# DeltaNet inverses by 8x8 blocks, stored by row, with all their multiplications on VectorE

## The chip, the core and the metric

The kernel runs on one core of one Trainium2 chip. A core has five engines with queues of their own: TensorE (PE in the profile; PEld are its weight loads), VectorE (DVE), ScalarE (ACT), GpSimd (POOL) and SyncE (SP, which issues the loads). Each engine works through its queue in order and waits at semaphores for the others. The metric is the device time of one execution in microseconds (us); the median over runs counts.

## The reference

Two layers, each made of a feed-forward network, a mixer and a second feed-forward network, over 256 tokens of width 1024. The mixer has three kinds of heads: window attention (6), differential attention (4) and a gated delta rule (6, in both directions). The change is in the delta rule alone. For each head, direction and chunk of 64 tokens it solves a unit lower triangular system:

```python
m_low = jnp.where(tril_strict, jnp.einsum('bhncd,bhnsd->bhncs', kb, kc) * decay, 0.0)
a_mat = jnp.eye(C, dtype=f32) + m_low
u = lax.linalg.triangular_solve(a_mat, vb, left_side=True, lower=True, unit_diagonal=True)
w = lax.linalg.triangular_solve(a_mat, kb * jnp.exp(gc)[..., None], left_side=True,
                                lower=True, unit_diagonal=True)
```

With 6 heads, 2 directions and 4 chunks there are 48 matrices of 64x64 in each layer.

## The kernel before

The kernel does not solve the systems; it inverts the matrices. Each 64x64 matrix is cut into two diagonal blocks of 32x32 and one block below them. The 96 diagonal blocks of a layer are laid one to a partition (four groups of 32 partitions, 24 used in each), so that one VectorE instruction works on all of them. `inv_start` gathers them into Dg, partly with VectorE's 32x32 transpose and partly with ScalarE copies, and transposes Dg into L; Vi is to become the inverse. Every step of the inversion is a call of `products`: one multiplication (TENSOR_TENSOR, line 799) of two broadcast views into the scratch tile pr, and one reduction over its last dimension (TENSOR_REDUCE, line 800). Each needs the one before.

- `inv_row` (ORDER's "ir"): the two 16x16 diagonal blocks of the 32x32, row by row, i = 1 to 15. Step i multiplies 2·i·i elements.
- `inv_off` ("io", n = 0 to 5): the block below them, by products of 1024 elements: three of L with Vi into pp, three of Vi with pp into Vi.
- `inv_end` ("ie"): transposes and copies of the result into WA and W, which TensorE then uses to complete the 64x64 inverse (`off1`, `off2`) and to run the scan over chunks.

L holds a block so that going along the summed index steps by 32 elements; Vi is read along consecutive elements in the row steps and in the first three "io" steps.

The set SHARED names the operations that go to GpSimd instead of VectorE: of the inversion the multiplications of rows 2, 4 and 11 (v2, v4, v11) and of the fifth "io" step (u4). Others in the set are additions of the convolution (t1, t7, t8, line 548) and of the differential heads (d0 to d3, line 729).

The table ORDER says in which order the mixer's pieces are written down; a scheduler then merges them into the queues, so that an engine's order is near to the table but not the same. Around the inversion stand: "p:9" to "p:16", projections for the attention heads, each of 8 matmuls (line 428, tile pj); "d", differential scores (lines 708 and 713, tile pss); "w", window scores (lines 669 and 675, also pss); "h" and "hw", heads' outputs. Projections and scores are written into the same pool of two PSUM buffers, "pm". A projection's buffer is free when VectorE has taken it out (dqk line 662, wq line 659). A differential score's buffer is free when VectorE has taken its maximum (mxd, line 716) and ScalarE has read it through two exponentials (line 719). Weights come by SyncE loads, up to seven ahead of their use.

Of the kernel before, what the change touches and what calls it, by code (L numbers as in the profile page):

```python
# [35 lines left out]
ORDER = """  # L36
A:0 A:1 A:2 K N A:3 G V c:1:0 c:1:1 clear c:0:0 c:1:2 GS co:1:0 c:0:1 co:1:1 co:1:2 ce:1 GE GT E:1 qn:1 co:0:0 co:0:1
c:0:2 co:0:2 ce:0 qn:0 E:0 E:3 qc:1:1 c:2:0 c:2:1 E:2 qc:0:0 qc:1:0 X:0:0 qc:0:1 ic X:1:1 X:0:1 X:1:0 i ir:1:2 ir:2:3
ir:3:4 ir:4:5 ir:5:6 p:15 ir:6:7 ir:7:8 ir:8:9 ir:9:10 ir:10:11 ir:11:12 ir:12:13 ir:13:14 c:2:2 ir:14:15 p:14 p:13
co:2:0 p:16 d:0 ir:15:16 d:2 co:2:1 io:0 co:2:2 p:9 d:1 p:12 d:3 w:0 io:1 h:2 h:1 p:10 h:0 io:2 io:3 h:3 p:11 w:1 w:2  # L40
hw:0 io:4 io:5 ie ce:2 dn hw:1 f g:0 hw:2 g:1 sa:0 sb:0 oT:3:4 sc:0 sa:1 sb:1 sc:1 sa:2 sb:2 sc:2 sa:3 sc:3 z:0 z:1
z:2 z:3 ze on:1 o:0:0 on:0 o:0:1 o:0:2 o:0:3 o:0:4 o:0:5 o:0:6 oT:7 oT:5:6 o:0:7 o:1:0 o:1:1 o:1:2 o:1:3 o:1:4 o:1:5
o:1:6 o:1:7
"""

NRAW = 8
# [3 lines left out]
    p2="pt", pk="pd", px="pt", pS="pt", po="pd", pw="pd", pT="pd", pso="pd", pto="pd",  # L50
)

SHARED = set("O2 S2 d0 d1 d2 d3 g5 s3 t1 t7 t8 u4 v11 v2 v4 x0 x4 x5".split())
C_M0, C_M1, C_DD, C_WD, C_SEL = 0, 64, 128, 640, 1152
NCONSTB = 1176

# [1 line left out]
class Kernel:  # L58
# [296 lines left out]
    def mixer(self, l, gnext):  # L355
# [22 lines left out]
        with ExitStack() as ctx:  # L378
# [4 lines left out]
            st = {}  # L383
# [13 lines left out]
            oT = tile_([P, KD, S], "oT")  # L397
# [130 lines left out]
            def conv(a, b):  # L528
# [15 lines left out]
                act(cv, pad[:, 0:S], AF.Copy, scale=cw[:, i * 5 : i * 5 + 1])  # L544
                if f"t{i}" in SHARED:
                    tap = self.sp.tile([P, S], F32, tag="sqt", name="tap")
                    act(tap, pad[:, 1 : S + 1], AF.Copy, scale=cw[:, i * 5 + 1 : i * 5 + 2])
                    gtt(cv, cv, tap, ALU.add)
                for w in range(2 if f"t{i}" in SHARED else 1, 5):
                    stt(cv, pad[:, w : w + S], cw[:, i * 5 + w : i * 5 + w + 1], cv, ALU.mult, ALU.add)  # L550
                st["cv", a, b] = cv

            def conv_out(a, b):
# [6 lines left out]
                cs = mt.tile([P, S], F32, tag="cs", name="cs")  # L560
                pool = f"s{a * 3 + b}" in SHARED
                if pool:
# [32 lines left out]
            def qk_channels(a, p):  # L595
# [4 lines left out]
                for e in range(2):  # L600
                    for half in range(2):
                        (nc.vector.tensor_copy if ("kq", a, half) in SHARED else nc.scalar.copy)(
                            kq[HALF[half], p, e:6:2, 1 - a, :],
# [60 lines left out]
            def win_scores(b):  # L664

                banks = [bank("pss") for j in range(2)]
                for j, pss in enumerate(banks):
                    if f"g{j * 3 + b}" in SHARED:
                        mm(pss, lhsT=self.wdiag[j * 3 + b], rhs=self.wd.rearrange("p a t -> p (a t)"), start=True, stop=False)
                for p in range(2):  # L670
                    c = slice(p * P, (p + 1) * P)
                    for j, r in enumerate(HALF):
                        slope = f"g{j * 3 + b}" in SHARED
                        o = banks[j][:, p * S : (p + 1) * S]
# [114 lines left out]
            def blk(t, off, *dims):  # L789

                base = t.rearrange("p a b -> p (a b)")
                return bass.AP(
                    tensor=base.tensor, offset=base.offset + off, ap=[list(base.ap[0])] + [list(x) for x in dims]
                )

            def products(o, in0, in1, dims, neg, on):
                n = dims[0] * dims[1] * dims[2]
                pv = st["pr"][:, 0:n].rearrange("p (a c j) -> p a c j", a=dims[0], c=dims[1])
                (gtt if on in SHARED else tt)(pv, in0, in1, ALU.mult)
                nc.vector.tensor_reduce(o, pv, AX.X, ALU.add, negate=neg)  # L800
# [8 lines left out]
            def inv_start():  # L809
                Dg = st["Dg"]  # L810
                for v in range(2):
                    us = slice(v * 12, v * 12 + 12)
                    for b in range(4):
                        o_ = Dg[B32[b], :, us].rearrange("p c u -> p u c")
                        if (b < 2) == (v == 0):
                            nc.vector.transpose(o_, XE[B32[b], 0, us, B32[b % 2]])
                        else:
                            act(o_, XE[B32[b], 0, us, B32[b % 2]], AF.Copy)
                L = st["L"] = tile_([P, 32, 32], "L", "t4b")
                nc.vector.transpose(L, Dg)  # L820
                st["pr"] = tile_([P, 1024], "pr", "pr")
                st["pp"] = tile_([P, 16, 16], "pp")

            def inv_row(i0, i1):
                Vi, L = st["Vi"], st["L"]
                for i in range(i0, i1):
                    products(
                        blk(Vi, i, (528, 2), (32, i)),
                        blk(L, i, (528, 2), (0, i), (32, i)),
                        blk(Vi, 0, (528, 2), (32, i), (1, i)),  # L830
                        (2, i, i),
                        True,
                        f"v{i}",
                    )

            def inv_off(n):
                Vi, L, pp = st["Vi"], st["L"], st["pp"]
                if n < 2:
                    i0 = n * 8
                    products(  # L840
                        pp[:, i0 : i0 + 8, 0:8],
                        blk(L, 16 + i0, (1, 8), (0, 8), (32, 16)),
                        blk(Vi, 0, (0, 8), (32, 8), (1, 16)),
                        (8, 8, 16),
                        False,
                        f"u{n}",
                    )
                elif n == 2:
                    products(
                        pp[:, :, 8:16],  # L850
                        blk(L, 16 + 8 * 32, (1, 16), (0, 8), (32, 8)),
                        blk(Vi, 8 * 33, (0, 16), (32, 8), (1, 8)),
                        (16, 8, 8),
                        False,
                        f"u{n}",
                    )
                elif n == 3:
                    products(
                        blk(Vi, 16, (1, 8), (32, 16)),
                        blk(Vi, 528, (1, 8), (0, 16), (32, 8)),  # L860
                        blk(pp, 0, (0, 8), (1, 16), (16, 8)),
                        (8, 16, 8),
                        True,
                        f"u{n}",
                    )
                else:
                    c0 = (n - 4) * 8
                    products(
                        blk(Vi, 24 + c0 * 32, (1, 8), (32, 8)),
                        blk(Vi, 528 + 8, (1, 8), (0, 8), (32, 16)),  # L870
                        blk(pp, c0, (0, 8), (1, 8), (16, 16)),
                        (8, 8, 16),
                        True,
                        f"u{n}",
                    )
# [142 lines left out]
            def out_proj(part, d):  # L1018
# [20 lines left out]
                "clear": clear, "N": norm, "V": values, "G": gates, "GS": gate_sums, "GE": gate_exps, "GT": gate_rows,  # L1039
                "c": conv, "co": conv_out, "ce": conv_end, "qn": qk_norm, "qc": qk_channels,  # L1040
                "E": decay, "X": products_kq, "K": constants, "p": att, "hw": win_out, "w": win_scores, "d": diff_scores, "h": head_out,
                "dn": diff_norm, "oT": to_oT, "ic": inv_clear, "i": inv_start, "ir": inv_row, "io": inv_off, "ie": inv_end,
                "f": off1, "g": off2, "ze": gate_out, "sa": scan_a, "sb": scan_b, "sc": scan_c, "on": out_norm, "o": out_proj,
                "l": load, "A": lambda a: token_proj(NA, "pv", "A", a),
                "z": lambda a: token_proj(NB, "pz", "z", a),
# [3 lines left out]
            for item in ORDER.split():  # L1049
                w = item.split(":")  # L1050
# [4 lines left out]
                elif w[0] == "o":  # L1055
                    n = (5, 3)[int(w[1])]
# [6 lines left out]
            for item, rs in zip(ORDER.split(), reads):  # L1063
# [6 lines left out]
                w = item.split(":")  # L1070
# [165 lines left out]
```

## Time and profile before

| what | value |
|---|---|
| median of 3 runs | 1150.33 us (1150.1 to 1151.57) |
| profiled execution | 1153.34 us, of which span 1151.5 us |
| PE busy | 1110.3 us (96%) |
| DVE busy | 738.0 us (64%) |
| ACT busy | 522.9 us (45%) |
| POOL busy | 82.3 us (7%) |
| mean granted TensorE clock | 0.977 |
| layer 0's mixer, inversion from first product to Vc | 262.84 to 309.95 us |
| layer 1's, the same | 826.45 to 873.55 us |

Times in the views count from the span's start. A row of a timeline has start, duration, engine, source line, operation, output and inputs, and in brackets how long the engine was idle before and who ended that. A row of groups has count, busy us, mean ns and idle before. A row of stretches has the busy time of each engine, the granted clock of TensorE (1.00 is full speed) and what the loads moved. The matmul records of 32-bit data come in pairs: a projection of 8 matmuls shows 16.

### The profile page before, as it was taken

Reading aid. Unit: us, or ns where it says so; the run is one execution under the profiler, and the core shown is the slowest. Engines: PE = TensorE matmul, PEld = TensorE weight load, DVE = VectorE, ACT = ScalarE, POOL = GpSimd, SP = SyncE. Lnnn points to the kernel's source line nnn. Section 1 sums busy time; section 2 is a strip of 40 time slices with the busy share of each in tenths; the row PEclk is TensorE's granted clock in tenths of the full one; section 3 lists DMA queues with packets and bytes.
Section 4 is the critical chain, followed back from the end, with each engine's and each line's share of the span. In section 5 each row is a group of like instructions: output and inputs, shape, how many; then the busy total and the mean of one; then the engine's idle time right before and its main releaser. Section 6 shows DMA issues by size and latency. Waiting matters only on the chain. (4 is left out here: it accounts for less than half of the span.)

```text
span 1151.5 us, 21957 instructions
## 1 busy us (share of the span) xinstructions
PE 1110.3 (96%) x8970; PEld 1022.2 (89%) x8970; DVE 738.0 (64%) x1442; ACT 522.9 (45%) x967; POOL 82.3 (7%) x135
## 2 busy tenths in 40 slices
PE   7999999998899999999999999999988999999996
PEld 7999999776668999999999999988756689999996
DVE  7766654778747566666566666547786476666653
ACT  5545442263472454454444454415436435445441
POOL 0000011101201200000100000121020021000010
PEclk9999999998899999999999999999988999999998
DMA  9655653521123555565555565534211254556521
GB/s 332 213 182 186 201 168 115 164 77 53 51 61 111 198 174 181 184 202 184 181 180 183 182 199 184 161 125 128 79 50 37 75 184 155 185 184 203 184 97 37
DMA packets 49637, 173.64 MB, mean 151 GB/s; under 512 B 5504, under 2 KB 6784, under 8 KB 49536
## 3 DMA queue, kind: packets, MB, share of 16 engines
q1 hardware_dynamic: 49104, 171.64, 45.5%
q8 instruction: 70, 1.15, 0.4%
q10 hardware_dynamic: 432, 0.60, 0.1%
q14 instruction: 31, 0.25, 0.1%
HBM read 171.17 MB, written 1.05 MB: 150 GB/s over the span
## 5 line engine op out<-in xcount | busy, mean ns | idle before, releaser
L254 DVE TENSOR_TENSOR wl<-wr,wh 128x1024 fp32r<-128x1024 f32 x254 | 311.7, 1228 | 172.5 <-ACT wh L253 172.0
L259 PE MATMUL ps<-xh,wh 128*128 128x256 f32 x1336 | 379.6, 284 | 0.8 <-ACT wh L253 0.8
L261 PE MATMUL ps<-xh,wl 128*128 128x256 f32 x1336 | 379.0, 284 | 0.8 <-DVE wl L254 0.8
L253 ACT ACTIVATE wh<-wr 128x1024 fp32r<-128x1024 f32 x254 | 267.2, 1053 | 246.6 <-issue 144.6
L260 PE MATMUL ps<-xl,wh 128*128 128x256 f32 x1336 | 378.7, 283 | 0.0
L259 PEld LDWEIGHTS ps<-xh,wh 128*128 128x128 f32 x1336 | 257.1, 192 | 1.6 <-ACT wh L253 1.0
L261 PEld LDWEIGHTS ps<-xh,wl 128*128 128x128 f32 x1336 | 257.0, 192 | 1.2 <-DVE wl L254 1.2
L260 PEld LDWEIGHTS ps<-xl,wh 128*128 128x128 f32 x1336 | 257.1, 192 | 0.0
L261 PE MATMUL ps<-hh,wl 128*128 128x256 f32 x672 | 187.9, 280 | 0.0
L260 PE MATMUL ps<-hl,wh 128*128 128x256 f32 x672 | 187.7, 279 | 0.0
L259 PE MATMUL ps<-hh,wh 128*128 128x256 f32 x672 | 187.6, 279 | 0.0
L428 PE MATMUL pj<-xf,wr 128*128 128x256 f32 x544 | 133.6, 402 | 2.9 <-issue 2.6
L260 PEld LDWEIGHTS ps<-hl,wh 128*128 128x128 f32 x672 | 126.3, 188 | 0.0
L261 PEld LDWEIGHTS ps<-hh,wl 128*128 128x128 f32 x672 | 126.1, 188 | 0.0
L259 PEld LDWEIGHTS ps<-hh,wh 128*128 128x128 f32 x672 | 125.9, 187 | 0.0
L428 PEld LDWEIGHTS pj<-xf,wr 128*128 128x128 f32 x544 | 107.6, 203 | 20.0 <-issue 3.3
L191 POOL TENSOR_TENSOR sqacc<-sqacc,sqt 128x256 f32<-128x256 f32 x41 | 34.6, 843 | 733.0 <-ACT sqt L187 732.9
L282 ACT ACTIVATE hh<-h 128x256 fp32r<-128x256 f32 x88 | 36.1, 416 | 90.4 <-DVE h L280 90.4
L277 DVE TENSOR_TENSOR t<-ps,f_rb 128x256 f32<-128x256 f32 x88 | 36.9, 424 | 37.9 <-PE ps L261 37.7
L1024 PE MATMUL py<-oT,wr 128*128 128x256 f32 x256 | 58.9, 384 | 0.0
L283 DVE TENSOR_TENSOR hl<-h,hh 128x256 fp32r<-128x256 f32 x88 | 36.8, 423 | 30.5 <-ACT hh L282 30.5
L1024 PEld LDWEIGHTS py<-oT,wr 128*128 128x128 f32 x256 | 47.2, 190 | 7.0 <-DVE x L1031 0.4
(321 smaller groups left out, 1128.5 us busy)
## 6 DMA issues: line engine op xcount, KB each, us to landing
wr<-in_ffn SPq DMA_DIRECT2D x258, 512.0 KB, 3.4
wr<-in_mix SPq DMA_DIRECT2D x50, 512.0 KB, 3.5
wr<-in_mix SPq DMA_DIRECT2D x8, 408.0 KB, 3.2
wr<-in_mix SPq DMA_DIRECT2D x8, 384.0 KB, 3.0
x<-in_x SPq DMA_DIRECT2D x4, 256.0 KB, 4.1
ar<-in_ffn SPq DMA_DIRECT2D x8, 128.0 KB, 3.9
cb<-in_constb SPq DMA_DIRECT2D x1, 588.0 KB, 10.1
out_y<-fo SPq DMA_DIRECT2D x2, 256.0 KB, 2.4
```

The costliest lines, as they stand in the source:

```text
L191: (eng or nc.gpsimd).tensor_tensor(self.sq, self.sq, t, ALU.add)
L253: nc.scalar.activation(h, w, AF.Copy)
L254: nc.vector.tensor_tensor(lo, w, h.bitcast(F32), ALU.subtract)
L259: mm(out, lhsT=ah, rhs=bh, start=start, stop=False)
L260: mm(out, lhsT=ah, rhs=bl, start=False, stop=False)
L261: mm(out, lhsT=al, rhs=bh, start=False, stop=stop)
L277: nc.vector.tensor_tensor(t[:rows], gate, rb[:rows], ALU.mult)
L282: nc.scalar.activation(hh[:n, j, :], h[:n], AF.Copy)
L283: nc.vector.tensor_tensor(hl[:n, j, :], h[:n], hh[:n, j, :].bitcast(F32), ALU.subtract)
L428: mm(ps[:, 0:S], lhsT=w[:, k * P : (k + 1) * P], rhs=xf[:, k, :], start=k == 0, stop=k == KD - 1)
L1024: mm(ps[:, 0:S], lhsT=st["o", q // NBLK][:, c], rhs=oT[:, k, :], start=k == ks[0], stop=k == ks[-1])
```

## The change

`inv_row` works on four 8x8 diagonal blocks for i = 1 to 7, 4·i·i elements a step. A new piece `inv_mid` ("im", n = 0 to 3) joins them to 16x16 blocks: for each of two blocks one step that multiplies L with Vi into pp and one that multiplies Vi with pp into Vi, 512 elements each. `inv_off` joins the 16x16 blocks to 32x32 as before, with L read in its new layout. In `inv_start` the quarters that were transposed are copied and the other way round, so that L is stored by row and its summed index runs over consecutive elements. No name of the inversion is left in SHARED: all its multiplications are on VectorE. In ORDER the steps "ir:8:9" to "ir:15:16" go and "im:0" to "im:3" come; the other pieces keep their order.

```diff
-ir:3:4 ir:4:5 ir:5:6 p:15 ir:6:7 ir:7:8 ir:8:9 ir:9:10 ir:10:11 ir:11:12 ir:12:13 ir:13:14 c:2:2 ir:14:15 p:14 p:13
+ir:3:4 ir:4:5 ir:5:6 p:15 ir:6:7 ir:7:8 im:0 im:1 im:2 c:2:2 im:3 p:14 p:13 co:2:0 p:16 d:0 d:2 co:2:1 io:0 co:2:2 p:9
...
-SHARED = set("O2 S2 d0 d1 d2 d3 g5 s3 t1 t7 t8 u4 v11 v2 v4 x0 x4 x5".split())
+SHARED = set("O2 S2 d0 d1 d2 d3 g5 s3 t1 t7 t8 x0 x4 x5".split())
...
-                        if (b < 2) == (v == 0):
+                        if (b < 2) != (v == 0):
                             nc.vector.transpose(o_, XE[B32[b], 0, us, B32[b % 2]])
...
             def inv_row(i0, i1):
...
                     products(
-                        blk(Vi, i, (528, 2), (32, i)),
-                        blk(L, i, (528, 2), (0, i), (32, i)),
-                        blk(Vi, 0, (528, 2), (32, i), (1, i)),
-                        (2, i, i),
+                        blk(Vi, i, (264, 4), (32, i)),
+                        blk(L, 32 * i, (264, 4), (0, i), (1, i)),
+                        blk(Vi, 0, (264, 4), (32, i), (1, i)),
+                        (4, i, i),
...
+            def inv_mid(n):
+
+                Vi, L, pp = st["Vi"], st["L"], st["pp"]
+                a, step = n % 2, n // 2
+                if step == 0:
+                    products(
+                        blk(pp, a * 64, (1, 8), (8, 8)),
+                        blk(L, a * 528 + 8 * 32, (32, 8), (0, 8), (1, 8)),
+                        blk(Vi, a * 528, (0, 8), (32, 8), (1, 8)),
+                        (8, 8, 8),
+                        False,
+                        f"m{n}",
+                    )
+                else:
+                    products(
+                        blk(Vi, a * 528 + 8, (1, 8), (32, 8)),
+                        blk(Vi, a * 528 + 264, (1, 8), (0, 8), (32, 8)),
+                        blk(pp, a * 64, (0, 8), (8, 8), (1, 8)),
+                        (8, 8, 8),
+                        True,
+                        f"m{n}",
+                    )
...
-                        blk(L, 16 + i0, (1, 8), (0, 8), (32, 16)),
+                        blk(L, (16 + i0) * 32, (32, 8), (0, 8), (1, 16)),
...
-                        blk(L, 16 + 8 * 32, (1, 16), (0, 8), (32, 8)),
+                        blk(L, 16 * 32 + 8, (32, 16), (0, 8), (1, 8)),
```

In the dims of `blk` each pair is (step, count), the last one being summed. The changed kernel's line numbers are lower by one up to `inv_row` and higher by 23 behind `inv_mid`.

Three places in the queues show what moves. First VectorE in layer 0 around the fourth dqk eviction, that of the projection p:16. Before:

```order
L800 TENSOR_REDUCE Vi<-pr 128x2x10
L800 TENSOR_REDUCE Vi<-pr 128x2x11
L799 TENSOR_TENSOR pr<-L,Vi 128x288
L662 SCALAR_TENSOR_TENSOR dqk<-pj,m_rb 128x256
L800 TENSOR_REDUCE Vi<-pr 128x2x12
L799 TENSOR_TENSOR pr<-L,Vi 128x338
L716 TENSOR_REDUCE mxd<-pss 128x2
L800 TENSOR_REDUCE Vi<-pr 128x2x13
```

And in the changed kernel:

```order
L798 TENSOR_TENSOR pr<-L,Vi 128x512
L661 SCALAR_TENSOR_TENSOR dqk<-pj,m_rb 128x256
L799 TENSOR_REDUCE pp<-pr 128x8x8
L798 TENSOR_TENSOR pr<-Vi,pp 128x512
L715 TENSOR_REDUCE mxd<-pss 128x2
L799 TENSOR_REDUCE Vi<-pr 128x8x8
```

The eviction stands behind the second middle step's product instead of the product of row 12, and the first maximum behind the third middle step's product.

Second, VectorE from the eviction of p:12 (wq) to the first window score (sc), where the fifth "io" step (u4) lies. Before:

```order
L659 SCALAR_TENSOR_TENSOR wq<-pj,m_rb 128x256
L716 TENSOR_REDUCE mxd<-pss 128x2
L800 TENSOR_REDUCE Vi<-pr 128x8x8
L716 TENSOR_REDUCE mxd<-pss 128x2
L799 TENSOR_TENSOR pr<-Vi,pp 128x1024
L723 RECIPROCAL c_3247<-smd 128x2
L686 SCALAR_TENSOR_TENSOR sc<-wd,pss 128x512
```

And in the changed kernel:

```order
L658 SCALAR_TENSOR_TENSOR wq<-pj,m_rb 128x256
L715 TENSOR_REDUCE mxd<-pss 128x2
L798 TENSOR_TENSOR pr<-Vi,pp 128x1024
L715 TENSOR_REDUCE mxd<-pss 128x2
L799 TENSOR_REDUCE Vi<-pr 128x8x8
L722 RECIPROCAL c_3239<-smd 128x2
L685 SCALAR_TENSOR_TENSOR sc<-wd,pss 128x512
```

Between the two maxima (mxd) of differential head 3 stood the reduction that waits for GpSimd's product; now the product itself stands there, and the reduction behind the second maximum.

Third, GpSimd in the same part of layer 0. Before:

```order
L799 TENSOR_TENSOR pr<-L,Vi 128x8
L548 TENSOR_TENSOR pad<-pad,tap 128x256
L799 TENSOR_TENSOR pr<-L,Vi 128x32
L799 TENSOR_TENSOR pr<-L,Vi 128x242
L729 TENSOR_TENSOR sc<-sc 128x512 x3
L799 TENSOR_TENSOR pr<-Vi,pp 128x1024
L729 TENSOR_TENSOR sc<-sc 128x512
```

And in the changed kernel:

```order
L532 MEMSET pad 128x2
L533 MEMSET pad 128x2
L547 TENSOR_TENSOR pad<-pad,tap 128x256 x2
L728 TENSOR_TENSOR sc<-sc 128x512 x4
L1006 TENSOR_TENSOR Stmp<-SC,egl 128x384
```

The four products are gone, and the additions of the convolution and of the differential heads are all that is left of it there.

More of the change, by code (lines that the diff above doesn't have):

```diff
@@ L38 @@
 c:0:2 co:0:2 ce:0 qn:0 E:0 E:3 qc:1:1 c:2:0 c:2:1 E:2 qc:0:0 qc:1:0 X:0:0 qc:0:1 ic X:1:1 X:0:1 X:1:0 i ir:1:2 ir:2:3
-ir:3:4 ir:4:5 ir:5:6 p:15 ir:6:7 ir:7:8 ir:8:9 ir:9:10 ir:10:11 ir:11:12 ir:12:13 ir:13:14 c:2:2 ir:14:15 p:14 p:13
[L40 to L43, printed above, removed]
+ir:3:4 ir:4:5 ir:5:6 p:15 ir:6:7 ir:7:8 im:0 im:1 im:2 c:2:2 im:3 p:14 p:13 co:2:0 p:16 d:0 d:2 co:2:1 io:0 co:2:2 p:9
+d:1 p:12 d:3 w:0 io:1 h:2 h:1 p:10 h:0 io:2 io:3 h:3 p:11 w:1 w:2 hw:0 io:4 io:5 ie ce:2 dn hw:1 f g:0 hw:2 g:1 sa:0
+sb:0 oT:3:4 sc:0 sa:1 sb:1 sc:1 sa:2 sb:2 sc:2 sa:3 sc:3 z:0 z:1 z:2 z:3 ze on:1 o:0:0 on:0 o:0:1 o:0:2 o:0:3 o:0:4
+o:0:5 o:0:6 oT:7 oT:5:6 o:0:7 o:1:0 o:1:1 o:1:2 o:1:3 o:1:4 o:1:5 o:1:6 o:1:7
 """
@@ L1041, in mixer @@
                 "E": decay, "X": products_kq, "K": constants, "p": att, "hw": win_out, "w": win_scores, "d": diff_scores, "h": head_out,
-                "dn": diff_norm, "oT": to_oT, "ic": inv_clear, "i": inv_start, "ir": inv_row, "io": inv_off, "ie": inv_end,
+                "dn": diff_norm, "oT": to_oT, "ic": inv_clear, "i": inv_start, "ir": inv_row, "im": inv_mid, "io": inv_off, "ie": inv_end,
                 "f": off1, "g": off2, "ze": gate_out, "sa": scan_a, "sb": scan_b, "sc": scan_c, "on": out_norm, "o": out_proj,
```

## The prediction

> **What bounds it now.** Read first: busy time of each engine by stretches of layer 0's mixer, in us from the span's start (length; PE, PEld, DVE, ACT, POOL busy with instructions; granted clock; DMA).
>
> ```profile
> 300.00:320.00 20.00, 16.00 (x64) 12.76 (x64) 13.65 (x25) 10.90 (x31) 2.45 (x2) 0.74 0.08 26
> 320.00:345.00 25.00, 25.00 (x325) 16.05 (x327) 11.51 (x38) 19.19 (x51) 0.00 (x0) 1.00 0.22 65
> ```
>
> From 320 TensorE has no gap, so time is lost only before: up to 320 it waits and runs at a lower clock. Read second: the timelines of TensorE, VectorE and GpSimd there.
>
> ```profile
> 272.93 0.38 PE L708 MATMUL pss<-ddb,sdiag 128*128 128x512 bf16 x1 [1.49 <-DVE dqk L662]
> ...
> 275.70 0.58 PE L708 MATMUL pss<-ddb,sdiag 128*128 128x512 bf16 x1 [0.97 <-ACT sc L719]
> ...
> 280.97 6.05 PE L428 MATMUL pj<-xf,wr 128*128 128x256 f32 x16
> ...
> 291.22 3.62 PE L428 MATMUL pj<-xf,wr 128*128 128x256 f32 x16
> ...
> 304.20 2.07 PE L675 MATMUL pss<-wq 64*128 64x256 f32 x4 [4.00 <-ACT sc L719]
> 306.21 1.97 PE L759 MATMUL pso<-V,PT 128*128 128x64 f32 x8
> 307.97 6.18 PE L428 MATMUL pj<-xf,wr 128*128 128x256 f32 x16
> ```
> ```profile
> 296.56 0.68 DVE L716 TENSOR_REDUCE mxd<-pss 128x2 f32<-128x512 f32 x1
> 301.22 1.22 DVE L800 TENSOR_REDUCE Vi<-pr 128x64 f32<-128x1024 f32 x1 [3.98 <-POOL pr L799]
> 302.35 0.68 DVE L716 TENSOR_REDUCE mxd<-pss 128x2 f32<-128x512 f32 x1
> ```
> ```profile
> 297.49 3.69 POOL L799 TENSOR_TENSOR pr<-Vi,pp 128x1024 f32<-128x1024 f32 x1
> ```
>
> Projections (pj) and scores (pss) share the two buffers of the pool pm. Each score goes around a ring: TensorE writes, VectorE takes the maximum (L716), ScalarE reads it twice (L719), and only then may TensorE write there again. The inverses stand in VectorE's queue between the maxima. The costliest case: the product u4 takes GpSimd 3.69 us, VectorE stands still 3.98, the ready maximum waits behind it until 302.35, and TensorE until 304.20. Read third: the stretches' view again, in steps of 3.41 us laid where the clock changes (and two of layer 1).
>
> ```profile
> 272.07:275.48 3.41, 1.80 (x7) 0.96 (x7) 3.38 (x7) 0.85 (x4) 0.00 (x0) 1.00 0.15 59
> 275.48:278.89 3.41, 3.19 (x7) 1.40 (x6) 2.97 (x6) 1.84 (x8) 0.00 (x0) 0.50 0.00 0
> 278.89:282.31 3.42, 3.27 (x7) 2.19 (x8) 2.30 (x6) 2.48 (x9) 1.26 (x1) 0.50 0.01 2
> 282.31:285.72 3.41, 3.41 (x9) 2.70 (x9) 3.38 (x4) 0.36 (x2) 0.00 (x0) 0.50 0.00 0
> 285.72:289.13 3.41, 2.58 (x11) 1.54 (x10) 3.41 (x7) 0.92 (x3) 1.15 (x1) 1.00 0.18 55
> ...
> 299.37:302.79 3.42, 0.84 (x4) 0.31 (x2) 1.57 (x2) 0.00 (x0) 1.81 (x1) 1.00 0.00 0
> ```
> ```profile
> 825.03:828.44 3.41, 2.13 (x12) 1.72 (x11) 2.55 (x10) 0.91 (x2) 1.04 (x3) 1.00 0.36 115
> ...
> 835.27:838.68 3.41, 1.80 (x7) 0.96 (x7) 3.34 (x8) 0.43 (x2) 0.00 (x0) 1.00 0.24 94
> ```
>
> The clock falls to 0.50 after a stretch with 1.80 or 0.84 busy (1.61 idle or more), holds after one with 2.13 (1.28 idle), and a fall lasts three stretches. It is dear: 16 records of a projection take 6.05 or 6.18 us against 3.62.
>
> **The change part by part.** The inverses' rows between 262.8 and 311 (count, busy, mean ns, idle before) give the total:
>
> ```profile
> L799 DVE TENSOR_TENSOR pr<-L,Vi 128x1024 f32<-128x1024 f32 (+12 forms) x15 | 11.6, 775 | 0.2
> ...
> L800 DVE TENSOR_REDUCE Vi<-pr 128x64 f32<-128x1024 f32 (+16 forms) x18 | 8.5, 472 | 5.5 <-POOL pr L799 5.3
> ...
> L799 DVE TENSOR_TENSOR pr<-Vi,pp 128x1024 f32<-128x1024 f32 x2 | 3.9, 1940 | 0.0
> ...
> L800 DVE TENSOR_REDUCE pp<-pr 128x64 f32<-128x1024 f32 (+1 forms) x3 | 3.6, 1214 | 0.0
> ```
> ```profile
> L799 DVE TENSOR_TENSOR pr<-L,Vi 128x1024 f32<-128x1024 f32 x3 | 6.1, 2024 | 0.0
> ...
> L799 DVE TENSOR_TENSOR pr<-L,Vi 128x450 f32<-128x450 f32 x1 | 0.9, 912 | 0.0
> ...
> L800 DVE TENSOR_REDUCE Vi<-pr 128x30 f32<-128x450 f32 x1 | 0.6, 616 | 0.0
> ```
> ```profile
> L254 DVE TENSOR_TENSOR wl<-wr,wh 128x1024 fp32r<-128x1024 f32 x254 | 311.7, 1228 | 172.5 <-ACT wh L253 172.0
> ```
>
> VectorE now spends 11.6 + 8.5 + 3.9 + 3.6 = 27.6 us per layer and waits 5.3 for GpSimd. A reduction of n elements costs 0.15 + 0.00104n (616 and 1214 ns). Products that step through L by 32 elements cost 1.75 to 1.94 ns an element (1940; 912 to 2024). The nearest row with both operands in sequence is wl, 1228 ns for 1024, so 0.15 + 0.00105n. Products whose both operands now run in sequence, in runs of 8 or 16, have no row: they cost between these. I take the wl price, since a reduction over short runs shows no such penalty. The Trainium skill's page "SBUF — State Buffer", section "Door 1: The DMA port swizzle", says that reads within a 16-byte line run at full rate and a step beyond 4 fp32 pays; by it runs of 8 stay near the low end, and the sum is the same.
>
> Rows i = 1 to 7 are 4i² elements, 560 together: 1.6 us of products, 1.6 of reductions. The four middle steps of 512: two in sequence at 0.69, two that step through Vi at 1.05, and reductions of 0.69: 6.2. The six last steps: 3 x 1.23 + 3 x 1.94 + 6 x 1.21 = 16.8. Together 26.3 against 27.6. So taking over 4 of GpSimd's products costs VectorE nothing, and 5.3 of waits go. Swapping copy and transpose in the start moves four 32x384 pieces to each engine as before: nothing. No DMA moves. GpSimd keeps its additions.
>
> Now along the path of layer 0, walked by hand with the new order of VectorE's queue and the durations above. A time in brackets is that of before.
>
> - *The first gap.* The fourth dqk eviction no longer stands behind twelve row steps and a wait for GpSimd. By then VectorE has 2.5 us less to do (the seven short row steps and one middle step), but the eviction must also await TensorE's projection, so it ends near 271.3 and the second score bank starts near 271.4 (272.93). TensorE then runs out near 273.8. It waits for the first maximum, for ScalarE's copy of vtok, which now stands ahead of the exponentials, and for the two exponentials: until about 275.1 (275.70). A gap of 1.25 to 1.5 us remains.
> - *Up to p:9, with the clock held.* Two score banks took 5.27 at half clock (275.70 to 280.97); at 3.62/6.05 of that they take 3.2. ScalarE has the first bank read by then, so projection p:9 starts at 278.2: **2.8** earlier.
> - *Up to p:12.* p:9 takes 3.62 instead of 6.05: **2.4**. Its eviction, the two maxima of the next head and two last-step products go around the ring until p:12; one of those products, 0.8 cheaper, lies between. I count **0.5**; p:12 starts at 285.5 (291.22).
> - *u4.* From the first maximum of head 3 to the second it was 302.35 − 296.56 = 5.79. Now only the maximum, 0.68, and u4's product, 1.94, lie between, less 0.2 of overlap, and the reduction of 1.22 goes behind the second: 2.4. That is **3.4** more. TensorE goes on 1.2 after the second maximum ends, as before (303.03 to 304.20), so at 295.1 (304.20).
> - *The second fall.* With no gap of 4 us the clock stays: 2.07 + 1.97 + 6.18 = 10.2 become, at 3.62/6.05, 6.1, or 5.7 as the short matmuls overlap; 0.3 goes to VectorE's evictions: **4.2**. The lead at the end of p:10 is 13.3.
> - *ScalarE.* VectorE's inverse ends only some 6.6 earlier (27.6 + 5.3 − 26.3), and ScalarE's copies into W and WA stand behind its two transposes, ahead of PT and of w:1's exponentials. By its queue TensorE waits 0.55 and 0.9 us for PT near 304 and 307: **1.5** is given back. From there both engines have the work of before, ScalarE with 19.19 busy of 25.
>
> Sum with the clock held: 2.8 + 2.4 + 0.5 + 3.4 + 4.2 − 1.5 = **11.8 us a layer**. If the first fall remains, the two banks and p:9 stay at half clock: 0.8 and 0.2 instead of 2.8 and 2.4; VectorE's cheaper products then give 0.9 in place of 0.5, and the rest is the same: 0.8 + 0.2 + 0.9 + 3.4 + 4.2 − 1.5 = **8.0**.
>
> **Which of the two.** The gap of 1.25 to 1.5 lies between 1.28 (held) and 1.61 (fell), and of the places at which stretches of 3.41 can lie, six in ten hold it whole. I give a fall four chances in ten in each layer, so one of two is the likeliest: 11.8 + 8.0 = 19.8, say 20. Against the profiled execution's 1153.34 (span 1151.5 and 1.84 around it) this is 1133.3. That execution lies 3.0 above the median of the runs, 1150.33, to which I apply the same difference: **1130.3**.
>
> **Rivals.**
> - *The clock holds in both layers*, 23.6: **1126.7**, chance 0.26. For it: the gap may be 1.25. The Trainium skill, "TensorE: Matmul & The Clock Gate", section "HAM oscillation — how this bites in real kernels", warns of gaps above about 3.4 us only; by that rule this is the case, since none is left. The trace disagrees: the stretch of 272.07 has no gap over 1.49 in it, yet 0.50 follows.
> - *It falls in both*, 16: **1134.3**, 0.13.
> - *Runs of 8 cost the stepped price.* VectorE's 26.3 becomes some 30; of this 2.4 (three products of 0.8) lies in the ring after 278: 4.8 less than forecast, **1135.1**, 0.10.
> - *ScalarE's queue becomes the bound in the tail:* its two waits grow together above 1.3 in one stretch and the clock falls there: 4.2 a layer lost again, **1138.7**, 0.07.
> - *The change doesn't do what it says:* the ring's ScalarE half, not VectorE, sets it. Then p:9 and the rest stay: within 2 us of **1150**, 0.04. Against it: 3.98 of standstill with the bank ready.
> - *Slower:* VectorE answers sooner, TensorE gets its work in small pieces with gaps between, and the clock stays at 0.50 from 275 to 313. Between the two falls of now lie some 17 us at full clock, two lengths of a fall (10.24 us) less a little; a fall's length costs 4.5 (10.2 less 5.7), so 9.0, against the 6.6 that VectorE gains: 2.4 lost a layer, **1155**, 0.05. It decides when every stretch up to 306 keeps over 1.3 idle. Against it: p:9 and p:12 are 3.6 us each without a gap.
>
> Forecast 0.35. The range 1125 to 1139 takes in the first five. Faster by over 0.2% (2.3 us, about what a measurement of this kernel can tell) 0.91, within 0.04, slower 0.05.
>
> **What would show it.** No wait of VectorE for GpSimd at the inverses; 512-element products at 0.7 and 1.05, those of L at 1.23 us; the last maximum of head 3 some 9 us earlier; TensorE's 4.00 wait gone; granted clock 1.00 from 286 to 320 in both layers; the 275 fall in one of two. Wrong if the maxima still wait on VectorE for over 2 us, if runs of 8 cost 1.9 ns an element, or if ScalarE leaves TensorE idle after 303.

## The result, and the profile after

| | median (lowest to highest, runs) | ratio to before, 95% interval |
|---|---|---|
| before, same chip | 1150.95 us (1150.10 to 1151.87, 4) | |
| changed kernel | 1137.90 us (1136.61 to 1140.55, 4) | 0.9885 [0.9870, 0.9899] |

The change gains 13.0 us; 20 were forecast. The profiled execution took 1140.55 us, span 1138.8, mean granted clock 0.986 (before 1153.34, 1151.5, 0.977).

VectorE's rows of the inverses in layer 0 of the changed kernel, grouped by line and operation (count, busy, mean ns, idle before):

```profile
L798 DVE TENSOR_TENSOR pr<-Vi,pp 128x1024 f32<-128x1024 f32 (+1 forms) x5 | 8.1, 1628 | 0.0
L798 DVE TENSOR_TENSOR pr<-L,Vi 128x1024 f32<-128x1024 f32 (+8 forms) x12 | 6.8, 568 | 0.1
L799 DVE TENSOR_REDUCE Vi<-pr 128x64 f32<-128x512 f32 (+9 forms) x12 | 6.6, 553 | 0.2
L799 DVE TENSOR_REDUCE pp<-pr 128x64 f32<-128x512 f32 (+2 forms) x5 | 5.0, 995 | 0.0
```

The sum is 26.5 us (forecast 26.3), and the 5.3 us of waits for GpSimd are gone. VectorE's timeline around u4 there:

```profile
293.75 0.67 DVE L715 TENSOR_REDUCE mxd<-pss 128x2 f32<-128x512 f32 x1
294.34 2.12 DVE L798 TENSOR_TENSOR pr<-Vi,pp 128x1024 f32<-128x1024 f32 x1
296.38 0.69 DVE L715 TENSOR_REDUCE mxd<-pss 128x2 f32<-128x512 f32 x1
```

The two maxima of head 3 are now 2.63 us apart instead of 5.79. TensorE's timeline of layer 0, and in the second listing the same places of layer 1 from p:9 on:

```profile
275.57 0.38 PE L707 MATMUL pss<-ddb,sdiag 128*128 128x512 bf16 x1 [1.52 <-ACT sc L718]
...
279.53 5.73 PE L427 MATMUL pj<-xf,wr 128*128 128x256 f32 x16
...
288.43 3.72 PE L427 MATMUL pj<-xf,wr 128*128 128x256 f32 x16
...
298.24 1.13 PE L674 MATMUL pss<-wq 64*128 64x256 f32 x4 [0.71 <-ACT sc L718]
...
300.23 3.67 PE L427 MATMUL pj<-xf,wr 128*128 128x256 f32 x16
```
```profile
835.15 6.10 PE L427 MATMUL pj<-xf,wr 128*128 128x256 f32 x16
844.43 3.72 PE L427 MATMUL pj<-xf,wr 128*128 128x256 f32 x16
...
854.23 2.07 PE L674 MATMUL pss<-wq 64*128 64x256 f32 x4 [0.71 <-ACT sc L718]
...
857.99 4.91 PE L427 MATMUL pj<-xf,wr 128*128 128x256 f32 x16
```

The first fall of the clock is still there in both layers: p:9 takes 5.73 and 6.10 us. The 4-us hole ahead of w:0 has become 0.71 in both. Yet only layer 0 runs w:0 and p:10 at full clock; in layer 1 the same four records of scores take 2.07 instead of 1.13. The stretches of 3.41 us show why this was not foreseen (length; PE, PEld, DVE, ACT, POOL busy; granted clock; DMA):

```profile
273.39:276.81 3.42, 1.90 (x9) 0.96 (x7) 3.39 (x6) 2.80 (x10) 0.00 (x0) 1.00 0.05 18
276.81:280.22 3.41, 3.41 (x8) 1.86 (x8) 3.00 (x6) 1.63 (x6) 0.00 (x0) 0.50 0.00 0
...
297.29:300.70 3.41, 2.70 (x15) 2.09 (x16) 3.39 (x7) 2.55 (x9) 0.45 (x1) 1.00 0.00 0
...
850.24:853.66 3.42, 3.28 (x15) 2.01 (x14) 3.42 (x4) 2.04 (x9) 0.46 (x1) 1.00 0.25 99
```

After the last one the clock fell, with TensorE busy 3.28 of 3.42; after the one of 297.29, at the same work in layer 0, it held with 2.70 busy. The forecast's rule, a fall after 1.6 us of idle time, cannot be what decides. At the places of the forecast's sum, the lead over the kernel before, counted in each layer from the first product pr of the inverse (before 262.84 and 826.45, now 263.78 and 819.68):

| lead, us | forecast, clock held | forecast, first fall stays | layer 0 | layer 1 |
|---|---|---|---|---|
| start of p:9 | 2.8 | 0.8 | 2.4 | 2.7 |
| start of p:12 | 5.7 | 1.9 | 3.7 | 3.6 |
| second bank of w:0 | 9.1 | 5.3 | 6.9 | 6.8 |
| end of p:10 | 13.3 | 9.5 | 11.2 | 7.9 |
| first px of the scan | 11.8 | 8.0 | 9.0 | 7.3 |

The layers together gain 16.3 in these two executions; their spans differ by 12.7, because the parts that the change does not touch took 3.6 longer in this execution (0.9 up to the first pr, 1.35 between the layers, 1.35 behind). Such parts differ between executions of one kernel; the 13.0 of the medians is the result.

### The profile page after: what moved, and what is told of

It reads as the page before. It is cut to its first block, busy times and chain, and to the rows that moved or that the text cites. A ratio compares the mean times of both kernels' runs of the same rounds, so it can differ in the third digit from the quotient of the medians.

```text
span 1138.8 us, 21945 instructions
## 1 busy us (share of the span) xinstructions
PE 1103.7 (97%) x8970; PEld 1018.8 (89%) x8970; DVE 736.6 (65%) x1434; ACT 523.3 (46%) x967; POOL 75.6 (7%) x127
## 3 DMA queue, kind: packets, MB, share of 16 engines
HBM read 171.17 MB, written 1.05 MB: 151 GB/s over the span
## 4 chain that ended last, share of the span: by engine, by line
PE 80%; DVE 10%; issue 4%; ACT 4%; DMA 1%; POOL 1%; SPq 0%; DVEq 0%; ACTq 0%; POOLq 0%
PE ps L260 21%; PE ps L259 21%; PE ps L258 21%; PE py L1047 5%; PE pj L427 2%; DVE pad L549 2%; PE pz L438 2%; PE pv L438 1%; DVE pr L798 1%; DVE wl L253 1%; PE pso L749 1%; PE pss L712 1%; PE px L968 1%; DMA wr<-in_ffn 1%; DVE mxd L715 1%
## 5 line engine op out<-in xcount | busy, mean ns | idle before, releaser
L427 PE MATMUL pj<-xf,wr 128*128 128x256 f32 x544 | 130.1, 394 | 2.8 <-issue 2.8
L427 PEld LDWEIGHTS pj<-xf,wr 128*128 128x128 f32 x544 | 105.0, 198 | 19.0 <-issue 3.6
L276 DVE TENSOR_TENSOR t<-ps,f_rb 128x256 f32<-128x256 f32 x88 | 36.8, 423 | 37.7 <-PE ps L260 37.5
```

The costliest lines, as they stand in the source:

```text
L276: nc.vector.tensor_tensor(t[:rows], gate, rb[:rows], ALU.mult)
L427: mm(ps[:, 0:S], lhsT=w[:, k * P : (k + 1) * P], rhs=xf[:, k, :], start=k == 0, stop=k == KD - 1)
```

## The experiments

All were run against the kernel before on the same chip; the medians of before beside them, 1150.95 to 1151.56, agree so well that medians of different chips are compared below. "Half clock" is the time at 0.50 within the two mixers of the profiled execution, from the granted clock's changes.

| run | median (range, runs), us | ratio, 95% interval | half clock, us |
|---|---|---|---|
| before | 1151.0 (medians 1150.95 to 1151.56) | | 41.0 |
| changed kernel | 1137.90 (1136.61 to 1140.55, 4) | [0.9870, 0.9899] | 20.5 |
| u4_back | 1144.89 (1142.30 to 1146.18, 6) | [0.9923, 0.9951] | 37.5 |
| old_blocks | 1144.71 (1144.42 to 1146.99, 5) | [0.9934, 0.9959] | 27.3 |
| columns | 1144.98 (1143.34 to 1146.33, 5) | [0.9931, 0.9955] | 37.5 |
| fill128 | 1139.10 (1134.68 to 1139.87, 5) | [0.9850, 0.9900] | 20.5 |
| fill32 | 1138.96 (1138.84 to 1140.64, 5) | [0.9872, 0.9908] | 27.3 |
| order_only | 1141.39 (1137.78 to 1145.69, 6) | [0.9886, 0.9936] | 30.7 |
| bank_only | 1124.89 (1122.06 to 1129.02, 5) | [0.9749, 0.9793] | 0 |
| spread | 1124.52 (1122.54 to 1126.84, 4) | [0.9739, 0.9787] | 10.2 |
| tail | 1138.01 (1137.35 to 1138.07, 4) | [0.9865, 0.9894] | 23.9 |
| spread_tail | 1122.34 (1118.62 to 1123.70, 4) | [0.9720, 0.9758] | 0 |
| before_bank | 1140.24 (1137.39 to 1145.12, 6) | [0.9892, 0.9931] | 17.1 |
| stretches (the changed kernel's mixers, more work at the end) | 1777.83 (1 run) | | 27.3 |

### Which part of the change gains

**u4_back**: one product of the changed kernel goes back to GpSimd.

```diff
-SHARED = set("O2 S2 d0 d1 d2 d3 g5 s3 t1 t7 t8 x0 x4 x5".split())
+SHARED = set("O2 S2 d0 d1 d2 d3 g5 s3 t1 t7 t8 u4 x0 x4 x5".split())
```

> The changed kernel with one product, u4, given back to GpSimd. Theory A (u4 on VectorE is the larger part of the gain): the second maximum of head 3 waits again behind u4, 3.2 us a layer (5.79 from the first to the second maximum before, 2.63 now), and TensorE's gap before w:0 brings layer 0's second fall of the clock back, 4.2 us once, since layer 1 has its second fall already: 3.2 x 2 + 4.2 = 10.6 slower than the changed kernel, about 1148.5 us. Rival B (the earlier p:9 and the cheaper products carry the gain): TensorE is held by the softmax ring at that place anyway, and giving u4 back costs at most 1 us a layer: under 1140.

It is 7.0 slower than the changed kernel. VectorE's timeline between the maxima of head 3:

```profile
293.17 0.68 DVE L715 TENSOR_REDUCE mxd<-pss 128x2 f32<-128x512 f32 x1
297.83 1.22 DVE L799 TENSOR_REDUCE Vi<-pr 128x64 f32<-128x1024 f32 x1 [3.98 <-POOL pr L798]
298.96 0.68 DVE L715 TENSOR_REDUCE mxd<-pss 128x2 f32<-128x512 f32 x1
```

The wait is back, 3.98, and with it 5.79 between the maxima and a fall of 10.24 us at w:0 of layer 0. Theory A holds in kind; 10.6 was too much. The layers lose 5.8 and 3.7 in this execution, 9.5 together, and 7.0 by the medians. With 37.5 us at half clock against 20.5, that is the wait and the falls together.

**old_blocks**: the kernel before, with its four products taken from GpSimd and nothing else.

```diff
-SHARED = set("O2 S2 d0 d1 d2 d3 g5 s3 t1 t7 t8 u4 v11 v2 v4 x0 x4 x5".split())
+SHARED = set("O2 S2 d0 d1 d2 d3 g5 s3 t1 t7 t8 x0 x4 x5".split())
```

> The kernel before with its block steps and its columns, but v2, v4, v11 and u4 on VectorE. Theory A: nearly all of the gain is the end of the waits for GpSimd. VectorE takes about 3.1 us of products (16, 64 and 484 elements, and 1.94 for u4) and loses 5.3 of waits, so it gains 2.2 a layer by queue, and at u4 the 3.2 a layer with layer 0's second fall: about 10 us faster than before, 1139 to 1142. Rival B: the row steps i = 8 to 15 on VectorE now stand ahead of the score maxima, the first gap grows, and the falls stay: 1146 to 1150.

6.3 faster than before, between the two forecasts: A's mechanism carries half of the gain, not nearly all of it.

**columns**: the changed kernel with L stored by column; every queue has the order of the changed kernel.

```diff
-                        if (b < 2) != (v == 0):
+                        if (b < 2) == (v == 0):
...
-                        blk(L, 32 * i, (264, 4), (0, i), (1, i)),
+                        blk(L, i, (264, 4), (0, i), (32, i)),
...
-                        blk(L, (16 + i0) * 32, (32, 8), (0, 8), (1, 16)),
+                        blk(L, 16 + i0, (1, 8), (0, 8), (32, 16)),
```

> The changed kernel with L stored by column as before, the order of all queues the same, so that only the price of the products with L differs. Those of 512 go from 0.69 to about 1.05 us, those of 1024 from 1.21 to about 2.0, the seven rows together 0.45 more: 3.6 us of VectorE a layer, of which 2.4 stand in the ring after 278. Theory A (VectorE's share of the ring counts one for one there): 2.4 x 2 = 4.8 slower than the changed kernel, 1142 to 1144. Rival B (ScalarE's half of the ring hides them): within 1.5 us of the changed kernel.

7.1 slower, more than either theory said. The products with L in the grouped rows of layer 0, each form apart, first of columns and then of the changed kernel:

```profile
L798 DVE TENSOR_TENSOR pr<-L,Vi 128x1024 f32<-128x1024 f32 x3 | 6.0, 1988 | 0.0
...
L798 DVE TENSOR_TENSOR pr<-L,Vi 128x512 f32<-128x512 f32 x2 | 2.1, 1026 | 0.1
```
```profile
L798 DVE TENSOR_TENSOR pr<-L,Vi 128x1024 f32<-128x1024 f32 x3 | 3.8, 1265 | 0.0
...
L798 DVE TENSOR_TENSOR pr<-L,Vi 128x512 f32<-128x512 f32 x2 | 1.4, 692 | 0.1
```

With the rows of i = 1 to 7, VectorE spends 3.2 us more a layer (10.0 against 6.8), 6.4 in all. Counted from pr, columns is behind the changed kernel by 2.0 us at p:9 in both layers and by 2.9 and 3.3 at the second bank of w:0: about one for one up to there, also ahead of the ring. At the first px it is 3.2 in layer 1 but 5.0 in layer 0, where w:0 now falls too. So the 7.1 holds the price and a share of falls (37.5 us at half clock against 20.5), and the runs do not separate the two. Taken together, three runs split the 13.0, each with the falls that came with it: products away from GpSimd 6.3 (old_blocks); blocks of 8 without the storage by row, nothing (columns, 1144.98, against old_blocks, 1144.71); the storage by row 7.1.

### What decides the clock

Here each record of a matmul gets a **weight**: its columns, times 4 for fp32 or 1 for bf16, times the share of the 128 rows that it uses, in units of one record of an fp32 matmul of 128 rows and 256 columns (such a matmul shows two). Sixteen of these records fill a stretch of 3.41 us. The forecast's own stretches separate by weight too: 2.5 and 1.7 fell, 8.7 held (825.03 of before, 2.13 busy); and 850.24 of the changed kernel, which fell, has 5.8, since its scores use 32 and 64 rows; 297.29, which held, has 5.9.

**stretches**: long pure streams of one kind, ahead of the last norm.

```diff
+        for what in "128 32 128 64 128 c32 128 bf 128 48 128 n64 128 tr 128 96 128".split():
+            for n in range(64 if what == "128" else 96):
...
+                if what.isdigit():
+                    r = int(what)
+                    nc.tensor.matmul(ps[:, 0:S], lhsT=w[0:r, :], rhs=v[0:r, :], start=True, stop=True)
```

> The changed kernel with TensorE work added ahead of the last norm, back to back and without gaps, its results used by nobody: 64 fp32 matmuls of 128 rows x 256 columns between each two of 96 matmuls that use 32 rows, 64 rows, 32 output columns, bf16 of 512 columns, 48 rows, three times 64 columns, two transposes, 96 rows. It asks what the clock is granted by. Theory of the prediction (idle time of TensorE, 1.6 of 3.41 us or more): there is no idle time, so the clock stays at 1.00 through all. Theory W (the columns streamed in a stretch of 3.41 us, each matmul weighted with the share of the 128 rows that it uses; the clock falls below about 36% of a full stream of fp32, since the three traces' stretches separate there): it falls to 0.50 in the 32-row part (25%), holds in the 64-row (50%) and the 48-row part just (37.5%), and holds with 32 output columns. Theory V (weighted with rows and output columns): it falls with 32 output columns too.

Stretches of that run: the last two before the clock falls in the 32-row part and the part behind them, 64 rows, the one before the fall in the 48-row part and the part behind it, 32 output columns:

```profile
1150.57:1153.98 3.41, 3.41 (x16) 2.74 (x15) 0.00 (x0) 0.00 (x0) 0.00 (x0) 1.00 0.00 0
1153.98:1157.39 3.41, 3.41 (x17) 2.94 (x16) 0.00 (x0) 0.00 (x0) 0.00 (x0) 1.00 0.00 0
1157.39:1235.91 78.52, 78.52 (x185) 60.72 (x185) 0.00 (x0) 0.00 (x0) 0.00 (x0) 0.50 0.00 0
1263.00:1303.00 40.00, 40.00 (x187) 34.64 (x187) 0.00 (x0) 0.00 (x0) 0.00 (x0) 1.00 0.00 0
1450.95:1454.36 3.41, 3.41 (x18) 2.95 (x17) 0.00 (x0) 0.00 (x0) 0.00 (x0) 1.00 0.00 0
1454.36:1526.00 71.64, 71.64 (x169) 54.89 (x167) 0.00 (x0) 0.00 (x0) 0.00 (x0) 0.50 0.00 0
1332.00:1372.00 40.00, 40.00 (x187) 20.42 (x186) 0.00 (x0) 0.00 (x0) 0.00 (x0) 1.00 0.00 1
```

TensorE is busy without a gap throughout. With 32 rows (weight 4) and 48 rows (6) the clock falls one stretch after the part begins and stays at 0.50 to its end; with 64 rows (8) it holds, and so it does with 32 output columns, 96 rows, bf16, 64-column matmuls and transposes. The idle theory and theory V fall. Theory W holds, with the bound a little higher than it said: 48 rows were expected to hold just.

**fill128** and **fill32**: the same question inside the mixer. Three matmuls whose results nobody reads, two of them in the gap of 1.5 us behind ptr; the second kernel differs from the first in the row count alone.

```diff
-                    transp(st["tr", a][p][:, b * P : (b + 1) * P], cp_)
+                    transp(st["tr", a][p][:, b * P : (b + 1) * P], cp_); (a, b, p) == (2, 2, 1) and fl(cp_, 3, 128)
...
+            fl = lambda w, n, r: [mm(o[:, 0:512], lhsT=w[0:r, :], rhs=xf[0:r, 2 * k : 2 * k + 2, :].rearrange("p a t -> p (a t)")[:, 0:512], start=True, stop=True) for o in [bank("px")] for k in range(n)]
```

> The changed kernel with three fp32 matmuls of 128 rows x 512 columns added in each layer, their results used by nobody: two right behind the last transposes of ptr, where TensorE idles 1.5 us, one ahead of p:9, where it idles 0.65. Some later rows of the tail change places. Theory W (the clock is granted by the columns streamed in a stretch of 3.41 us, weighted with the rows in use, and falls below about 3/8 of a full fp32 stream, where the 48-row part of the stretches run fell and the 64-row part held): a stretch of about 2,560 of 16,384 gets 4,096 more, the first fall goes in most places at which the stretches can lie, and the kernel gains 3 to 4 us a layer where it goes: 1130 to 1135 us. Idle theory (1.6 of 3.41 us idle): the gap is filled, the fall goes too: 1130 to 1132. Rival (the added matmuls stand ahead of scores that are waited for): 1 to 2 slower than the changed kernel, 1139 to 1140.

> The same kernel as fill128, row for row in all queues, but the three added matmuls use 32 of the 128 rows: the same TensorE time, a quarter of the weight. Theory W: a stretch of 2,560 gets only 1,024 more and stays under 6,144, so the first fall remains in both layers, and this kernel is 4 to 7 us slower than fill128. Idle theory: TensorE is as busy as in fill128, so the two are the same within 1 us.

The stretches that hold the filled gap, layers 0 and 1, and the one behind each, first of fill128, then of fill32:

```profile
271.25:274.66 3.41, 3.41 (x13) 1.62 (x12) 3.38 (x6) 2.69 (x10) 0.00 (x0) 1.00 0.13 52
274.66:278.08 3.42, 2.79 (x9) 1.05 (x7) 3.42 (x8) 1.43 (x7) 0.32 (x1) 1.00 0.01 2
827.62:831.03 3.41, 3.41 (x14) 1.62 (x13) 3.38 (x6) 1.88 (x7) 0.00 (x0) 1.00 0.26 100
831.03:834.45 3.42, 3.42 (x12) 1.72 (x11) 3.39 (x8) 1.43 (x7) 0.00 (x0) 1.00 0.00 0
```
```profile
271.13:274.54 3.41, 3.41 (x12) 1.43 (x10) 3.41 (x5) 2.52 (x9) 0.00 (x0) 1.00 0.13 53
274.54:277.96 3.42, 3.42 (x11) 1.94 (x9) 2.83 (x7) 1.42 (x5) 0.15 (x1) 0.50 0.01 2
827.50:830.92 3.42, 3.42 (x11) 1.58 (x11) 3.39 (x6) 2.81 (x10) 0.00 (x0) 1.00 0.05 18
830.92:834.33 3.41, 3.32 (x10) 1.33 (x8) 2.55 (x7) 1.50 (x5) 0.51 (x1) 0.50 0.01 2
```

Equally busy, 3.41 of 3.41. With 128 rows (weights 10.5 and 11.1) the clock holds in both layers, with 32 rows (4.3 and 4.2) it falls in both. The clock does what theory W said. **The time does not**: the two kernels take the same 1139. TensorE's timeline of fill128 shows the first reason:

```profile
278.64 3.72 PE L427 MATMUL pj<-xf,wr 128*128 128x256 f32 x16 [1.19 <-ACT sc L718]
```

At full clock the score banks are done sooner, but p:9 needs a buffer of pm that ScalarE has not yet read, so it starts 16.9 us behind pr in both kernels and both layers. (In the changed kernel it is 15.8 and 15.5. The added matmuls also moved VectorE's queue: a product of 1.23 us now stands ahead of that buffer's maximum, which begins 14.9 behind pr in layer 0 instead of 13.5. So the pair shows the clock, but its time against the changed kernel does not price a held clock.) The second reason: w:0's stretch came to a weight of 5.1 in both layers of fill128 and fell for 10.24 us each time; in fill32 it fell in layer 1 alone, and layer 0 had a fall of 3.41 us at p:12. Counted from pr, fill128 reaches w:0 2.5 and 1.0 us sooner, but the first px at 73.2 and 72.9 against 72.1 and 73.9. One fall was exchanged for another, and the times forecast for the pair, 1130 to 1135 for fill128 and 4 to 7 more for fill32, both failed.

### TensorE's buffers

**spread**: another order, and the projections p:9 to p:12 in a PSUM pool that is free there. **bank_only** and **order_only** have one of the two edits each.

```diff
-                ps = bank("pj")
+                ps = bank("pj" if i in (*range(9), 13, 14, 15, 16) else "px")
...
-p:16 d:0 d:2 co:2:1 io:0 co:2:2 p:9 d:1 p:12 d:3 w:0 io:1 h:2 h:1 p:10 h:0 io:2 io:3 h:3 p:11
+p:16 d:0 co:2:1 io:0 co:2:2 p:9 d:2 p:12 d:1 io:1 p:10 d:3 w:0 h:2 h:1 h:0 io:2 io:3 h:3 p:11
```

> The changed kernel in another order: the projections p:9, p:12 and p:10 each between two heads of the score matmuls (d:0 p:9 d:2 p:12 d:1 p:10 d:3), and p:9 to p:12 in the PSUM pool pt, whose two buffers are free there, so that a projection waits for no exponential. Theory W: no 3.41 us without full-row matmuls are left up to d:3; the first fall goes in both layers (3 to 4 us each) and TensorE no longer stands still for ScalarE ahead of p:9 (0.65) or for the scores' banks; what is left is w:0: 1128 to 1133 us. Rival (the ring of VectorE and ScalarE, not TensorE, sets the end of head 3; the scores of d:2 only come later): 1137 to 1142.

> The order of the spread run (d:0 p:9 d:2 p:12 d:1 p:10 d:3) with the projections in the pool pm as in the changed kernel. Theory W (rows in use): from d:1 on no long narrow part is left, but p:9 still waits for the first bank of d:0 to be read, so 4.7 us of narrow work and idle time stand ahead of p:9 and the first fall stays in most places: about half of the 13 us that spread gained on the changed kernel, 1130 to 1134 us. Rival (the PSUM pool carries the gain): within 2 us of the changed kernel, 1136 to 1140.

> The PSUM pool of the spread run (p:9 to p:12 in pt) with the order written as in the changed kernel; TensorE's queue then has the first matmuls of p:9 behind ptr, ahead of d:2. Theory W: those two full-row matmuls and no wait for a bank ahead of p:9 take away part of the first gap, the rest of the narrow work still lies together: 1131 to 1135 us. Rival (the order carries the gain): 1136 to 1139.

The pool is the whole of it: bank_only 1124.89, 13.0 faster than the changed kernel. The order alone is no faster (3.5 slower by the medians, the intervals overlap): p:9 ahead of d:2 waits for the same exponentials and now keeps d:2 waiting. I had put about half on the order; that was wrong, and bank_only came out below both of its ranges, as spread did below its own. TensorE's timeline of bank_only:

```profile
274.31 1.03 PE L427 MATMUL px<-xf,wr 128*128 128x256 f32 x4
275.27 0.38 PE L707 MATMUL pss<-ddb,sdiag 128*128 128x512 bf16 x1
...
278.01 2.43 PE L427 MATMUL px<-xf,wr 128*128 128x256 f32 x10
280.27 0.38 PE L707 MATMUL pss<-ddb,sdiag 128*128 128x512 bf16 x1
280.58 0.69 PE L712 MATMUL pss<-dqk 32*128 32x256 f32 x2
...
282.58 3.72 PE L427 MATMUL px<-xf,wr 128*128 128x256 f32 x16
```

The projections (now px) lie wherever a score waits for its bank. They fill the gaps and bring rows: no fall is left in either mixer. Of the 13.0, the 20.5 us at half clock account for up to 10 by estimate (half of them). The rest agrees with the waits: from 263 to 330 TensorE waits 4.3 us against 6.3 in the changed kernel, 2 less in layer 0. A stretch of the same run, idle for 1.52 us, near the 1.61 at which the clock of the kernel before fell:

```profile
310.45:313.86 3.41, 1.89 (x9) 0.83 (x7) 2.56 (x10) 3.13 (x12) 0.00 (x0) 1.00 0.01 2
```

Only 1.89 busy, but full rows, weight 7.0, and the clock holds.

**before_bank**: the same line in the kernel before.

> The kernel before (blocks of 16, columns, u4 on GpSimd) with the one line of bank_only: p:9 to p:12 in the pool pt. It asks whether the 13 us of the change and the 13 us of the pool are the same time. Theory S (they add: the change shortens VectorE's queue and takes away the wait at u4, the pool takes away TensorE's waits for banks and the narrow stretches): about 13 less than before, 1137 to 1140 us, with the 4-us hole at u4 partly filled by p:10, which no longer needs a scores' bank. Theory O (they overlap: with projections free to run, TensorE no longer waits for VectorE's inverse): 1125 to 1130, and the change is worth little beside the pool.

10.8 faster than before, and the change on top of it gains another 15.4 (1140.24 to 1124.89). The two add: theory S, with 1140.24 at the end of its range. The wait at GpSimd's u4 remains there: a two-element instruction of VectorE (line 724) lasts 3.32 us, to the end of u4's product. It shows up later, where TensorE waits for the transposed scores:

```profile
303.99 0.32 PE L759 MATMUL pso<-V,PT 128*128 128x64 f32 x1 [3.75 <-ACT PT L741]
```

### ScalarE in the tail

**tail** and **spread_tail**: four copies into W go from ScalarE to VectorE.

```diff
-                        (nc.vector.tensor_copy if b < 2 else nc.scalar.copy)(
+                        (nc.vector.tensor_copy if b < 2 else nc.vector.tensor_copy)(
```

> The changed kernel with ScalarE's four copies into W (inv_end, b = 2 and 3) given to VectorE. Theory (the prediction's term: ScalarE's queue in the tail gives back 1.5 us a layer, since those copies stand ahead of PT and of w:1's exponentials): 1 to 1.5 faster a layer, 1135 to 1136 us. Rival (VectorE, with its own maxima of w:1 and w:2 there, becomes late instead, or TensorE's projections cover the waits): within 1 us of the changed kernel.

> The spread run with the same four copies given to VectorE. Theory as in tail: 2 to 3 faster than spread, 1121.5 to 1122.5. Rival: TensorE is hardly waiting for ScalarE there any more (1.4 us in the layer for PT), so within 1 us of spread's 1124.5.

On the changed kernel nothing (+0.1), so the theory failed there. On spread 2.2 us by the medians, but the intervals of the two ratios overlap. What ScalarE's queue costs in the tail stays open; spread_tail is the fastest kernel of these runs, 29.2 us under the kernel before on the same chip (1151.56).

## Why the prediction forecast half as much again as came

**Right.** The products' prices: 0.69, 1.03 and 1.27 us against 0.69, 1.05 and 1.23, total 26.5 against 26.3. The waits for GpSimd are gone. *u4*: 3.4 forecast, 3.2 in both layers (6.9 − 3.7 and 6.8 − 3.6; the product took 2.12, not 1.94); u4_back puts it back. *Up to p:12* with the fall staying: 0.2 + 0.9 forecast, 1.3 and 0.9 measured.

**Right in size by luck.** *Up to p:9*: 2.4 and 2.7 in the table come close to the 2.8 for a held clock, though the clock fell. It fell late: only the last score bank ahead of p:9 ran at half clock, not the last two. ScalarE's last read of the first of these banks ends 15.2 us behind pr in both layers, and p:9 started 18.1 behind pr before, so a held clock could have given at most 2.9. In u4_back, tail and the stretches run, whose queues are the same up to there, the fall begins earlier, p:9 stands 16.4 to 16.9 behind pr, and the gain is 1.3 to 1.8.

**The step that failed** is the rule of the clock, and with it two terms. "Which of the two" took the fall as a matter of 1.25 to 1.5 us of gap, four chances in ten a layer; the weight of those stretches is 2.6 and 2.4, far under the bound of about 6, and they fall however the gap turns out. No layer held, so the 2.4 of *p:9 at full clock* did not come. And *the second fall*, "with no gap of 4 us the clock stays", 4.2 in each layer: 4.3 came in layer 0 (11.2 − 6.9), 1.1 in layer 1 (7.9 − 6.8), where the same work, lying otherwise to the stretches, weighs 5.8 and falls for 6.8 us. Layer 0 escaped narrowly, with 5.9; in the stretches run, with the same mixers, the fall comes at w:0 of layer 0. "A fall lasts three stretches" was wrong too: in the mixers of these runs one to four.

**Off in size, and half in reason.** *ScalarE's queue*, −1.5: −2.2 in layer 0, −0.6 in layer 1. TensorE's timeline of layer 0 there, with two waits that the kernel before does not have:

```profile
308.08 1.10 PE L758 MATMUL pso<-V,PT 128*128 128x64 f32 x8 [1.14 <-ACT PT L740]
...
317.86 2.20 PE L438 MATMUL pz<-wr,xf 128*128 128x384 f32 x6 [1.28 <-DVE sc L685]
```

The wait of 1.14 for PT is the one forecast, and layer 1 has none. The other, 1.28 and in layer 1 1.18, is for VectorE, which the term left out; tail, which relieves ScalarE alone, gained nothing.

So both layers went the way of "it falls in both" (16.0 of gain; 16.3 measured in the profiled pair), with a part of the second fall kept in one of them. The medians show 3 less. The stretches run, a second execution of the same mixers, leads by 6.0 and 8.6 at the first px, 14.6 together, and its falls lie otherwise. The rest is not explained by a mechanism: single executions of one kernel differ by up to 8 us (order_only), the times of untouched parts differ too, and two profiled executions do not show the mean.

Two slips in the working left the forecast as it was. The 1940 ns given for products with L belong to pr<-Vi,pp. And 17 us at full clock are 1.7 lengths of a fall, so the slower rival would have lost 7.5 − 6.6 = 0.9 a layer, not 2.4.

The rival drawn from the Trainium skill, "TensorE: Matmul & The Clock Gate", section "HAM oscillation — how this bites in real kernels" (only gaps above about 3.4 us), fails as the trace already said: the clock fell after 850.24 with 0.14 us idle, and in fill32 with none. "Runs of 8 cost the stepped price" is answered by the rows (692 ns for 512); columns shows what it would have cost, 7.1 with its falls rather than the 4.8 that was allowed for. The rival of ScalarE's queue gives nearly the measured time, 1138.7, but by another mechanism: no fall in the tail is in the trace.

## What to carry to other kernels

Before arguing from a gap of TensorE, ask which buffer the next matmul waits for: here a second pool for four projections was worth about as much as the whole rewrite of the inverse, and the two added up. Here the clock followed how many rows the matmuls of 3.41 us used, not how busy the engine looked, and full-row work between narrow scores kept it up (bank_only). A product that reads its operand in sequence instead of in steps costs VectorE a third less here, and that was about half of the gain (7.1 of 13.0, falls included).

## What the hardware showed that was not expected

The clock follows the columns streamed times the rows in use. In the fourteen traces of this case (behind the first 60 us and ahead of the last 15), 4,388 stretches of 3.41 us began at full clock. The 44 after which it fell have weights of 0.0 to 5.95 out of 16; the 4,344 after which it held have 5.15 and more. By busy time they cannot be told apart: falls came with up to 3.41 busy, and it held with as little as 1.89. The weight counts rows and not output columns: the part with 32 output columns held for all its 40 us. Between 5.15 and 6.0 both happen. Part of that lies in the weight itself: a bf16 record of 512 columns takes as long as an fp32 record of 256 (0.22 us each in the stretches run), and if it counts as much, 1 instead of 0.5, the span in which both happen shrinks to 5.88 to 6.06. Whether what is left is the modelled ends of the matmuls or the rule itself stays open.
